# A fused transformer layer on one core: modulation computed a tile of features at a time, with keys and queries between the tiles

## The chip, the core and the metric

The kernel runs on one core of one Trainium2 chip. The core has five engines with instruction queues of their own: TensorE (PE in the profile, with PEld for its weight loads), VectorE (DVE), ScalarE (ACT), GpSimd (POOL) and SyncE (SP), which here only issues DMAs. Each engine works through its queue in order, and semaphores hold an instruction back until what it needs is there. The metric is the device time of one execution in microseconds (us). The kernel before took a median of 1546.04 us in 3 runs, 1545.74 to 1547.45.

## The reference, cut to what matters

One layer takes 256 latent tokens `x` and 256 context tokens `ctx`, each with 2048 features, in float32. The part around the change:

```python
mod = (jax.nn.silu(c) @ w_mod[l] + b_mod[l])[:, None, :]
sa, ca, ga, sm, cm, gm = jnp.split(mod, 6, axis=-1)
mod_c = jax.nn.silu(c_ctx) @ w_mod[l] + b_mod[l]
sa_c, ca_c, ga_c, sm_c, cm_c, gm_c = jnp.split(mod_c, 6, axis=-1)
h_c = modulate(x_ctx, norm_attn_w[l], sa_c, ca_c)   # rmsnorm(x, w) * (1 + scale) + shift
k_c = rmsnorm(split_qk(p_c_kv[..., :QK_WIDTH]), k_norm_w[l])      # p_c_kv = h_c @ w_in[..]
h = modulate(x, norm_attn_w[l], sa, ca)
p = h @ w_in[l]
q = axial_rope(rmsnorm(split_qk(p[..., Q_OFF:K_OFF]), q_norm_w[l]), row, col)
k = axial_rope(rmsnorm(split_qk(p[..., K_OFF:V_OFF]), k_norm_w[l]), row, col)
```

After that come values, attention, a pooling mixer, gates, an output product and an MLP of width 8192. No product of `h` can start for a block of 128 features before the shift `sa` and the scale `ca` of that block are known, and these are a product of a vector with 2048 x 256 weights.

## The kernel before, in words

**Precision.** A weight chunk is 128 x 1024 float32 (512 KB). For the large products it is split into a high part (`whi`, or `first` for the first keys; a cast on ACT, L212) and a low part (`wlo`; a subtraction on DVE, L213), and every product is three matmuls (L240 to L242, or L414 to L417 further on). The weights of the modulation are used as they were loaded.

**The first stage** makes the modulation and, beside it, the first 512 columns of keys and queries. It is `layer` from `sb = bank("ssq")` to `steps(100)`.

- There are 16 tiles of 128 features (here f0 to f15). Tile f needs four chunks of `w_m`. `mod_half` (L351) multiplies two chunks on PE into the bank `mod`: four narrow matmuls a chunk, each on 32 columns of the array; a trace counts every one twice.
- `mod_rows` copies the result out (`rows`, ACT, L356), two tiles at once; `mod_columns` turns it into columns with tiny matmuls (`modT`, PE, L365), copies them (`col`, L368) and adds bias and weight on DVE (L371 to L373); `hidden` makes `hL` (latents) or `hC` (context) of the tile from them: DVE L384, ACT L385, DVE L386.
- `pair_steps` yields steps of three matmuls (128 x 512 each). A pair of tiles needs 12: four for keys of the latents ("kx"), four for queries ("q"), four for keys of the context ("kc"). `steps(n)` puts n of them between the halves of modulation.
- `square_sums` (ACT L463, DVE L464, PE L465) and `rsq` make the norms, once for `x` at the start, once for `ctx` in tile 4.

**What sets the order.** The code is recorded in program order, and a scheduler then orders each engine's queue; where `pin` is used (for a few instructions), program order is kept. Loads come from one list (`stream`, filled by `plan`), and `wchunk` runs ahead of their use by 3 chunks. All DMAs go through SP's queue, in order; a DMA that has no free buffer holds all behind it. Chunks have five buffers (tag `raw`), for `w_m` and for the rest alike. Other tags: `w2` (nine buffers of 2 KB a partition: `rows`, `hw`, `sq`), `s8` (two of 8 KB: `cv`, the vectors of the conditioning, and `prq`, the tables), `aT` (two of 4 KB; the norms `rms` in this stage).

**Later stages.** Values (`v`), more queries and keys with attention beside them, pooling, gates, the output product, the MLP. A second list of chunks (`late_gen`: `w_ga`, `w_cm`, `w_sm`, `w_gm`) is summed up on DVE beside them, at a rate set by credits that each load gives; `late_split` splits a finished sum.

Of the kernel before, what the change touches and what calls it, by code (L numbers as in the profile page):

```python
# [32 lines left out]
for _n, _w in (("ident", 128), ("c", 16), ("cc", 16), ("bsa", 16), ("bca", 16), ("nw", 16),  # L33
               ("pscale", 8), ("subln", 1), ("edge", 60)):
    PRM[_n] = (_o, _o + _w)
    _o += _w
# [12 lines left out]
def layer(ctx: ExitStack, tc, a, out):  # L49
# [5 lines left out]
    ordered = [False]  # L55

    class Engine:


        def __init__(self, engine):  # L60
            self.engine = engine

        def __getattr__(self, name):
            emit = getattr(self.engine, name)
            return (lambda *a, **k: pin(emit(*a, **k))) if ordered[0] else emit

    act, vec = Engine(nc.scalar), Engine(nc.vector)
# [13 lines left out]
    def small(name, n):  # L81
        return pool.tile([P, n], F32, tag="sm", name=name, bufs=12)
# [28 lines left out]
    def raw_chunk(src, n=1024):  # L111
        raw = pool.tile([P, n], F32, tag="raw", name="raw", bufs=5)
        nc.sync.dma_start(raw, src)
        return raw
# [14 lines left out]
    besides = {(2, 2): [("cT", 0)], (3, 0): [("cT", 1)], (3, 2): [("cT", 2)], (4, 0): [("cT", 3)], (7, 0): [("prq",)]}  # L129
    for m in range(1, 8):  # L130
        kq = (("w_k", 0, m - 1), ("w_q", 0, m - 1))
        if m == 3:
            besides[7, 1] = kq
        else:
            besides[2 * m, 1], besides[2 * m, 3] = kq[:1], kq[1:]
# [47 lines left out]
    done = [0]  # L183

    def load_next():
# [14 lines left out]
        raw = raw_chunk(src, n)  # L200
        if key[0] == "w_m":
            loaded.append((key, raw, raw))
            return
        if key[:2] == ("w_k", 0):
# [39 lines left out]
    def rsq(v, n, div, tag=None):  # L244

        mk = (lambda nm: small(nm, n)) if n <= 16 else (lambda nm: work(nm, [P, n]))
        y = pool.tile([P, n], F32, tag=tag, name=tag, bufs=2) if tag else mk("rq_y")
# [42 lines left out]
    cv = s8("cv", [P, 4, KT, 32])[:, 0]  # L290
# [3 lines left out]
    quads = pool.tile([P, 2], F32, tag="quads", name="quads")  # L294
    vec.reduce_sum(quads, ident.rearrange("p (j c) -> p c j", j=4)[:, 0:2, :], axis=AX.X)
    b1 = small("b1", 16)
    vec.tensor_scalar(b1, pr("bca"), 1.0, None, ALU.add)

# [42 lines left out]
    def mod_half(f, half, ps):  # L341

        raws = [wchunk("w_m", f, 2 * half + i, ahead=FIRST_AHEAD)[0] for i in range(2)]
        c = (f % 2) * T
        for i in range(2):
            for j in range(4):
                k = 8 * half + 4 * i + j  # L350
                pe.matmul(ps[32 * j:32 * j + 32, c:c + T], cv[:, k, :], raws[i][:, j * T:j * T + T],  # L351
                          start=k < 4, stop=k >= 12)

    def mod_rows(ps, f, n):
        rows = work("rows", [P, n * T])
        act.copy(rows, ps[:, (f % 2) * T:(f % 2) * T + n * T])  # L356
        return rows

    def mod_columns(f, rows, n):

        pt = bank("modT")
        for i in range(n):
            for a in range(2):
                o = 2 * (a * n + i)
                pe.matmul(pt[:, o:o + 2], rows[:, (2 * i + a) * P:(2 * i + a) * P + P], quads,  # L365
                          start=i + a == 0, stop=i == n - 1 and a == 1, skip_group_check=True)
        col = small("col", 8)
        act.copy(col[:, 0:4 * n], pt[:, 0:4 * n])  # L368
        c3 = col[:, 0:4 * n].rearrange("p (i c) -> p i c", c=2)
        ks = slice(f, f + n)  # L370
        vec.tensor_add(c3[:, 0:n, :], c3[:, 0:n, :], b1[:, ks].unsqueeze(2).broadcast_to([P, n, 2]))  # L371
        vec.tensor_mul(c3[:, 0:n, :], c3[:, 0:n, :], pr("nw")[:, ks].unsqueeze(2).broadcast_to([P, n, 2]))
        vec.tensor_add(c3[:, n:2 * n, :], c3[:, n:2 * n, :], pr("bsa")[:, ks].unsqueeze(2).broadcast_to([P, n, 2]))  # L373
        return c3

    def hidden(k, t, c3, n=2):

        src, h = ((xT, hL), (cT, hC))[t]
        hw = work("hw", [P, n, T])
        for kk in range(n):  # L380
            ht, k8 = h[(k + kk) // 8], (k + kk) % 8
            u = hw[:, kk, :]
            bias = c3[:, n + kk, t:t + 1]
            vec.scalar_tensor_tensor(u, src[:, k + kk, :], c3[:, kk, t:t + 1], rms[t], ALU.mult, ALU.mult)  # L384
            act.activation(ht[:, 0, k8, :], u, AF.Identity, bias=bias)  # L385
            vec.scalar_tensor_tensor(ht[:, 1, k8, :], u, bias, ht[:, 0, k8, :].bitcast(F32), ALU.add, ALU.subtract)  # L386
# [36 lines left out]
    def qk_evac(ps, tt, g, dest, tab, wait):  # L423
# [9 lines left out]
        m1 = work("qm1")  # L433
        m3 = m1.rearrange("p (h d) -> p h d", d=64)
        if tt < 2:
            vec.tensor_mul(m3, r3, tabs[:, tab, tt, :].unsqueeze(1).broadcast_to([P, 8, 64]))
            m2 = work("qm2")
            for ax in range(2):
                for b in range(2):
                    o = ax * 32 + b * 16  # L440
                    i = ax * 32 + (1 - b) * 16
                    vec.tensor_mul(m2.rearrange("p (h d) -> p h d", d=64)[:, :, o:o + 16], r3[:, :, i:i + 16],
                                   tabs[:, tab + 1, tt, o:o + 16].unsqueeze(1).broadcast_to([P, 8, 16]))
            gp.tensor_add(m1, m1, m2)
        else:
            vec.tensor_mul(m3, r3, wkt.unsqueeze(1).broadcast_to([P, 8, 64]))

        def turn():
            pt = bank("qkT")
            for i in range(4):  # L450
                pin(pe.transpose(pt[:, i * P:i * P + P], m1[:, i * P:i * P + P], ident))
# [32 lines left out]
    order = [("kx", 0), ("q", 0), ("kx", 1), ("q", 1), ("kc", 0), ("kc", 1), ("kx", 2), ("q", 2)]  # L484
    for j in range(3, 8):
        order += [("kc", j - 1), ("kx", j), ("q", j)]
    side = chain(*(pair_steps(*o) for o in order + [("kc", 7)]))

# [4 lines left out]
    def hold(w, j):  # L493
        held[w, j] = wchunk(w, 0, j, ahead=FIRST_AHEAD)
# [3 lines left out]
    def columns(ps, f, n):  # L498
        cols[f] = mod_columns(f, mod_rows(ps, f, n), n)

# [3 lines left out]
    rms = [rsq(sb[:, 0:T], T, P / D, "aT")]  # L504
    ps = bank("mod")
    for f in range(2):
        mod_half(f, 0, ps)
        if f == 1:
            columns(ps, 0, 1)
            hidden(0, 0, cols[0], 1)  # L510
        mod_half(f, 1, ps)
    before = mod_rows(ps, 1, 1)
    for m in range(1, 8):
        f = 2 * m
        ps = bank("mod")
        if m == 2:
            sb = bank("ssq")
        mod_half(f, 0, ps)
        n = 1 if m == 1 else 2
        cols[f - n] = mod_columns(f - n, before, n)  # L520
        hidden(f - n, 0, cols[f - n], n)
        if m != 3:
            hold("w_k", m - 1)
        if m == 3:
            hidden(2, 1, cols[2])
        steps(4 if m > 2 else 0)
        mod_half(f, 1, ps)
        if m != 3:
            hold("w_q", m - 1)
        if m == 2:  # L530
            for i in range(3):
                square_sums(cT, vec, sb, i)()
        if m > 3:
            hidden(f - 2, 1, cols[f - 2])
        steps(4 if m == 3 else 3)
        mod_half(f + 1, 0, ps)
        if m == 2:
            square_sums(cT, vec, sb, 3)()
            rms.append(rsq(sb[:, 0:T], T, P / D, "aT"))
        if m == 3:  # L540
            hold("w_k", 2)
            hold("w_q", 2)
            hidden(4, 1, cols[4])
        steps(4 if m == 3 else 3)
        if m == 7:
            columns(ps, 14, 1)
            hidden(14, 0, cols[14], 1)
        mod_half(f + 1, 1, ps)
        if m == 2:
            for i in range(2):  # L550
                hidden(i, 1, cols[i], 1)
        if m == 5:
            tables()
        if m < 7:
            steps(4 if m == 3 else 2)
            before = mod_rows(ps, 0, 2)
    columns(ps, 15, 1)
    hidden(15, 0, cols[15], 1)
    hold("w_k", 7)
    hold("w_q", 7)  # L560
    steps(2)
    for i in range(2):
        hidden(14 + i, 1, cols[14 + i], 1)
    steps(100)
# [52 lines left out]
    def late_split(acc, norm_w, o):  # L617
        for q in range(2):
            ah, al = work("ah", dt=F32R), work("al", dt=F32R)
            split(ah, al, acc[:, q * 512:q * 512 + 512])  # L620
            later(4 + q, partial(late_sum, ah, al, norm_w[q] if norm_w else None, o[:, q * 512:q * 512 + 512]))
# [411 lines left out]
def _layout(inp):  # L1033
# [37 lines left out]
    for w in WINDOWS:  # L1071
# [8 lines left out]
          "edge": np.broadcast_to(edge, (P, len(edge)))}  # L1080
# [36 lines left out]
```

## Time and profile before

| what | value |
|---|---|
| median of 3 runs | 1546.04 us |
| the profiled execution | 1545.81 us |
| its span, first to last instruction | 1543.3 us |
| mean granted clock of TensorE | 0.983 |
| PE busy | 1498.7 us, 97% of the span |
| DVE, ACT busy | 987.3 us (64%), 691.3 us (45%) |
| HBM read | 344.44 MB, 225 GB/s over the span |

The profile lists instructions with start and duration. A matmul's duration includes time in the pipeline, so consecutive matmuls overlap: what one costs is the distance from its start to the next one's start. "[1.20 <-ACT first L212]" behind an instruction says that the engine sat idle for 1.20 us before it, until the instruction of that name ended. A view by windows gives, for each stretch, the busy time of every engine, then the clock that was granted to TensorE (1.00 is full), the busy share of the DMA engines and what they moved in GB/s. A view of waits sums up who waited for whom.

### The profile page before, as it was taken

How to read it: one execution, taken by the hardware profiler on the slowest of the kernel's cores; microseconds unless marked ns; L12 is line 12 of the kernel's file. 1: busy time of each engine (PE TensorE's matmuls, PEld its weight loads, DVE VectorE, ACT ScalarE, POOL GpSimd, SP SyncE). 2: the span in 40 equal slices, each digit the busy share in tenths (PEclk: the TensorE clock that was granted, in tenths of full speed). 3: DMA queues.
4: the chain of work that ended last, by engine and by line, in shares of the span. 5: the costliest groups of instructions: out<-in, count | busy, mean ns of one | idle time of the engine just before them, and what ended most of it. 6: DMA issues, size and time to landing. Idle time of an engine off the chain costs nothing.

```text
span 1543.3 us, 20017 instructions
## 1 busy us (share of the span) xinstructions
PE 1498.7 (97%) x7592; PEld 1200.3 (78%) x7592; DVE 987.3 (64%) x1215; ACT 691.3 (45%) x944; POOL 120.5 (8%) x120
## 2 busy tenths in 40 slices
PE   6898999999999999999999999999999999999998
PEld 3554787768878888888879988888888888888887
DVE  2533778778877667666767665666666555555565
ACT  3322534556555434444444554544445453444432
POOL 0000011001240000000000100100000010000260
PEclk8898999999999999999999999999999999999999
DMA  9887578455658777788765777767777556566564
GB/s 366 289 292 250 191 237 281 152 177 192 201 175 305 245 263 262 247 280 286 232 191 169 227 237 242 230 213 238 231 240 227 201 187 185 189 189 188 183 190 137
DMA packets 97439, 347.84 MB, mean 225 GB/s; under 512 B 11072, under 2 KB 11712, under 8 KB 97344
## 3 DMA queue, kind: packets, MB, share of 16 engines
q1 hardware_dynamic: 96768, 345.49, 68.2%
q8 instruction: 59, 0.97, 0.2%
q0 software_dynamic: 576, 1.08, 0.2%
q14 instruction: 36, 0.29, 0.1%
HBM read 344.44 MB, written 2.10 MB: 225 GB/s over the span
## 4 chain that ended last, share of the span: by engine, by line
PE 94%; DVE 2%; ACT 2%; POOL 1%; DMA 1%; issue 1%; DVEq 0%; SPq 0%; ACTq 0%; POOLq 0%
PE f L966 14%; PE f L414 8%; PE f L417 8%; PE f L415 8%; PE f L969 7%; PE pg L417 4%; PE pg L415 4%; PE pg L414 4%; PE mod L351 2%; PE wo L415 2%; PE pyy L415 2%; PE v L417 2%; PE pyy L417 2%; PE wo L417 2%; PE v L415 2%; PE v L414 2%
## 5 line engine op out<-in xcount | busy, mean ns | idle before, releaser
L213 DVE TENSOR_TENSOR wlo<-raw,whi 128x1024 fp32r<-128x1024 f32 x443 | 547.5, 1237 | 377.7 <-ACT whi L212 361.3
L212 ACT CAST whi<-raw 128x1024 fp32r<-128x1024 f32 x443 | 462.6, 1045 | 594.1 <-PE f L415 188.1
L966 PE MATMUL f<-h,whi 128*128 128x512 f32 x896 | 226.9, 395 | 0.0
L414 PE MATMUL f<-whi,act 128*128 128x512 f32 x512 | 202.7, 396 | 0.0
L415 PE MATMUL f<-whi,act 128*128 128x512 f32 x512 | 201.7, 394 | 0.0
L966 PEld LDWEIGHTS f<-h,whi 128*128 128x128 f32 x896 | 160.9, 188 | 30.5
L615 DVE SCALAR_TENSOR_TENSOR macc<-raw,sil,macc 128x1024 f32<-128x1024 f32 x128 | 167.2, 1306 | 1.8 <-issue 1.6
L417 PE MATMUL f<-wlo,act 128*128 128x512 f32 x512 | 140.2, 395 | 0.0
L969 PEld LDWEIGHTS f<-h,wlo 128*128 128x128 f32 x896 | 122.5, 188 | 10.2
L969 PE MATMUL f<-h,wlo 128*128 128x256 f32 x896 | 124.5, 281 | 0.0
L417 PEld LDWEIGHTS f<-wlo,act 128*128 128x128 f32 x512 | 96.0, 187 | 23.5
L414 PEld LDWEIGHTS f<-whi,act 128*128 128x128 f32 x512 | 96.0, 187 | 23.4
L415 PEld LDWEIGHTS f<-whi,act 128*128 128x128 f32 x512 | 95.9, 187 | 22.8
L414 PE MATMUL pg<-whi,hL 128*128 128x512 f32 x256 | 101.6, 397 | 0.0
L415 PE MATMUL pg<-whi,hL 128*128 128x512 f32 x256 | 101.4, 396 | 0.0
L977 POOL TENSOR_TENSOR rsq<-relu 128x512 f32<-128x512 f32 x28 | 29.2, 1042 | 547.1 <-ACT relu L976 536.9
L417 PE MATMUL pg<-wlo,hL 128*128 128x512 f32 x256 | 70.2, 395 | 1.6 <-DVE wlo L213 1.6
L417 PEld LDWEIGHTS pg<-wlo,hL 128*128 128x128 f32 x256 | 47.9, 187 | 13.7 <-DVE wlo L213 2.0
L415 PEld LDWEIGHTS pg<-whi,hL 128*128 128x128 f32 x256 | 48.0, 188 | 11.8 <-issue 0.2
L414 PEld LDWEIGHTS pg<-whi,hL 128*128 128x128 f32 x256 | 48.0, 187 | 11.4 <-issue 0.2
L415 PE MATMUL wo<-whi,mix 128*128 128x512 f32 x128 | 50.7, 396 | 0.0
L414 PE MATMUL wo<-whi,mix 128*128 128x512 f32 x128 | 50.4, 394 | 0.0
(263 smaller groups left out, 2146.7 us busy)
## 6 DMA issues: line engine op xcount, KB each, us to landing
raw<-in_w_ff_dram SPq DMA_DIRECT2D x240, 512.0 KB, 4.2
raw<-in_w_m_dram SPq DMA_DIRECT2D x64, 512.0 KB, 4.9
raw<-in_w_ga_dram SPq DMA_DIRECT2D x32, 512.0 KB, 4.4
raw<-in_w_cm_dram SPq DMA_DIRECT2D x32, 512.0 KB, 4.5
raw<-in_w_gb_in_dram SPq DMA_DIRECT2D x32, 512.0 KB, 4.5
raw<-in_w_ga_in_dram SPq DMA_DIRECT2D x32, 512.0 KB, 4.6
raw<-in_w_sm_dram SPq DMA_DIRECT2D x32, 512.0 KB, 4.6
raw<-in_w_o_dram SPq DMA_DIRECT2D x32, 512.0 KB, 4.4
```

Source lines behind the costliest of these rows:

```text
L212: act.copy(hi, raw)
L213: vec.tensor_sub(lo, raw, hi.bitcast(F32))
L351: pe.matmul(ps[32 * j:32 * j + 32, c:c + T], cv[:, k, :], raws[i][:, j * T:j * T + T], start=k < 4, stop=k >= 12)
L414: pe.matmul(banks[t], tok(h, k, 0, tt), wt, start=k == 0, stop=False)
L415: pe.matmul(banks[t], tok(h, k, 1, tt), wt, start=False, stop=False)
L417: pe.matmul(banks[t], tok(h, k, 0, tt), wt, start=False, stop=k == 2 * nk - 1)
L615: pin(vec.scalar_tensor_tensor(acc, raw, sil[:, 0, k:k + 1], acc, ALU.mult, ALU.add))
L966: pe.matmul(ps, hi[:, kk * P:kk * P + P], both(h2, k), start=k == 0, stop=False)
L969: pe.matmul(ps[:, T:2 * T], lo[:, kk * P:kk * P + P], act_slice(h2, k, 0), start=False, stop=k == KT - 1)
L977: gp.tensor_mul(sq, r, r)
```

## The change

- **Modulation.** `mod_half` becomes `mod_tile`: all four chunks of a tile in one run. Rows, columns and hidden are made for one tile, no longer for two.
- **Steps.** `PACE` sets how many steps follow each tile: none for f0 and f1, then 4, 4, 6, 6, 8, 8, and 6 from f8 on. Half of them come ahead of `mod_columns`, half behind. The last 12 steps come at the end, interleaved.
- **Order on PE.** PE's instructions of this stage keep program order (`ordered_pe`; the wrapper shows as L67).
- **Buffers.** Chunks of odd tiles go into tiles that later stages use: two into one `s8` tile, two into the two `aT` tiles. Even tiles stay in `raw`, with the chunks of keys and queries. `cv` and the two `rms` move to `w2`.
- **Squares of ctx** are all in tile 4, behind its four chunks. `hidden` of the context is caught up in f4, f5 and f6, then runs with the tile.
- **Small things.** `quads` comes with the parameters; a bias needs two operations on DVE, not three; in `qk_evac` the rotated product is made in place, in two `w2` buffers, not four; `late_split` makes its second half two chunks later; the last pair of the stage runs ahead by one chunk, not three.

PE's queue, where the scheduler had put one pair of tiles. `mod` is the modulation, `modT` its turn into columns; `w_k_254` to `w_k_257` are the banks of keys (latents, then context), `w_q_283` and `w_q_284` those of queries. Before, from the middle of f10 on:

```order
L351 MATMUL mod<-raw,cv 32x256 x4
L240 MATMUL w_k_254<-first,hL_96 128x512
L240 MATMUL w_k_255<-first,hL_96 128x512
L240 MATMUL w_k_256<-first,hC_98 128x512
L351 MATMUL mod<-raw,cv 32x256 x4
L240 MATMUL w_k_257<-first,hC_98 128x512
L241 MATMUL w_k_254<-first,hL_96 128x512
L242 MATMUL w_k_254<-first,hL_96 128x512
L241 MATMUL w_k_255<-first,hL_96 128x512
L242 MATMUL w_k_255<-first,hL_96 128x512
L351 MATMUL mod<-raw,cv 32x256 x4
```

After, one whole tile (f10), where the banks of keys are 249 and 250 and those of queries 316 and 317:

```order
L67 MATMUL mod<-raw,cv 32x256 x16
L67 MATMUL w_k_249<-first,hL_93 128x512 x3
L67 MATMUL w_k_250<-first,hL_93 128x512 x3
L67 MATMUL w_k_249<-first,hL_93 128x512 x3
L67 MATMUL modT<-prm,rows 128x2 x2
L67 MATMUL w_k_250<-first,hL_93 128x512 x3
L67 MATMUL w_q_316<-whi,hL_93 128x512
L67 MATMUL w_q_316<-wlo,hL_93 128x512
L67 MATMUL w_q_316<-whi,hL_93 128x512
L67 MATMUL w_q_317<-whi,hL_93 128x512
L67 MATMUL w_q_317<-wlo,hL_93 128x512
L67 MATMUL w_q_317<-whi,hL_93 128x512
```

Four chunks stood in four places and now stand in one; in the whole stage the 64 chunks stood in 49 places and now stand in 16.

ACT's queue, where an odd tile's rows are copied and the next chunks of keys (`first`) and queries (`whi`) are cast. Before, a pair of tiles in the second half of the stage:

```order
L356 COPY rows<-mod 128x512
L368 COPY col<-modT 128x8
L385 ACTIVATE hL_96<-hw,col 128x256 x2
L385 ACTIVATE hC_98<-hw,col 128x256
L212 CAST first<-raw 128x1024
L385 ACTIVATE hC_98<-hw,col 128x256
L212 CAST whi<-raw 128x1024
```

After, the odd tile f11:

```order
L366 COPY rows<-mod 128x256
L224 CAST first<-raw 128x1024
L376 COPY col<-modT 128x4
L224 CAST whi<-raw 128x1024
L389 ACTIVATE hL_93<-hw,col 128x256
L389 ACTIVATE hC_95<-hw,col 128x256
```

The cast of the keys stood behind the hidden tiles and now stands ahead of the columns, right behind the rows of the odd tile.

SP's queue, with buffer numbers and with what each DMA waits for (PE, DVE: an earlier reader of the buffer; DMAHW: an earlier DMA). Before, a pair of tiles:

```order
L113 DMA raw_704<-in_w_k_dram 128x1024 [waits DMAHW7_49,PE_49]
L113 DMA raw_725<-in_w_m_dram 128x1024 [waits DMAHW0_49,PE_49]
L113 DMA raw_727<-in_w_m_dram 128x1024 [waits DMAHW1_49,PE_49]
L113 DMA raw_754<-in_w_q_dram 128x1024 [waits DMAHW2_49,PE_49]
L113 DMA raw_772<-in_w_m_dram 128x1024 [waits DMAHW3_49,PE_49]
L113 DMA raw_774<-in_w_m_dram 128x1024 [waits DMAHW4_49,DVE_49]
L113 DMA raw_784<-in_w_m_dram 128x1024 [waits DMAHW5_49,PE_49]
L113 DMA raw_802<-in_w_m_dram 128x1024 [waits DMAHW6_49,PE_49]
```

After, keys and queries of one pair, then f12 (four chunks) and the start of f13:

```order
L115 DMA raw_873<-in_w_k_dram 128x1024 [waits DMAHW4_49,PE_49]
L115 DMA raw_877<-in_w_q_dram 128x1024 [waits DMAHW5_49,DVE_49]
L212 DMA raw_883<-in_w_m_dram 128x1024 [waits DMAHW6_49,PE_49]
L212 DMA raw_903<-in_w_m_dram 128x1024 [waits DMAHW7_49,PE_49]
L212 DMA raw_905<-in_w_m_dram 128x1024 [waits DMAHW0_49,PE_49]
L212 DMA raw_941<-in_w_m_dram 128x1024 [waits DMAHW4_49,DMAHW1_49,DVE_49]
L212 DMA raw_943<-in_w_m_dram 128x1024 [waits DMAHW2_49]
L212 DMA raw_943<-in_w_m_dram 128x1024 [waits DMAHW3_49]
```

Nearly every chunk of `w_m` waited for PE. Now an odd tile's chunks (943) need no reader in the same pair, and an even tile's fourth chunk (941) waits for DVE: for the subtraction that ends the use of the keys' chunk 873.

The diff, cut to its core:

```diff
     for f in range(KT):
         for i in range(4):
             plan("w_m", f, i)
-            for key in besides.get((f, i), ()):
-                plan(*key)
-    plan("w_k", 0, 7)
-    plan("w_q", 0, 7)
+            if f in (2, 3) and i % 2 == 1:
+                plan("cT", 2 * f - 4 + i // 2)
...
+        j = 2 if f == 6 else -1 if f == 5 or f % 2 == 0 else f // 2
+        if j >= 0:
+            plan("w_k", 0, j)
+            plan("w_q", 0, j)
...
+    def mod_raw(f, i):
+        if f % 2 == 0:
+            return pool.tile([P, 1024], F32, tag="raw", name="raw", bufs=5)
+        if i > 1:
+            return pool.tile([P, 1024], F32, tag="aT", name="raw", bufs=2)
+        if i == 0:
+            wide[0] = s8("raw", [P, 2, 1024])
+        return wide[0][:, i, :]
...
-    def mod_half(f, half, ps):
-        raws = [wchunk("w_m", f, 2 * half + i, ahead=FIRST_AHEAD)[0] for i in range(2)]
+    def mod_tile(f, ps):
+        raws = [wchunk("w_m", f, i, ahead=FIRST_AHEAD)[0] for i in range(4)]
         c = (f % 2) * T
-        for i in range(2):
+        for i in range(4):
             for j in range(4):
-                k = 8 * half + 4 * i + j
+                k = 4 * i + j
                 pe.matmul(ps[32 * j:32 * j + 32, c:c + T], cv[:, k, :], raws[i][:, j * T:j * T + T],
...
+    PACE = (0, 0, 4, 4, 6, 6, 8, 8) + (6,) * 8
+    context = {4: (0, 1), 5: (2, 3, 4), 6: (5, 6)}
+    ordered_pe[0] = True
...
+    for f in range(KT):
+        if f % 2 == 0:
+            ps = bank("mod")
+        rows = mod_tile(f, ps)
+        if f == 4:
             sb = bank("ssq")
+            for i in range(4):
                 square_sums(cT, vec, sb, i)()
+            rms.append(rsq(sb[:, 0:T], T, P / D, "rms"))
+        if j >= 0:
+            for w in ("w_k", "w_q"):
+                held[w, j] = wchunk(w, 0, j, ahead=FIRST_AHEAD if j < 7 else 1)
+        steps(PACE[f] // 2)
+        cols[f] = mod_columns(f, rows)
+        steps(PACE[f] - PACE[f] // 2)
+        hidden(f, 0, cols[f])
+        for k in context.get(f, (f,) if f > 6 else ()):
+            hidden(k, 1, cols[k])
...
+    lasts = [pair_steps(n, 7) for n in ("kx", "q", "kc")]
+    for _ in range(2):
+        for g in lasts:
+            next(g)
+            next(g)
+    ordered_pe[0] = False
```

More of the change, by code (lines that the diff above doesn't have):

```diff
@@ L125, in plan @@
         stream.append(((name,) + idx, rate))
[L129 to L135, printed above, removed]
     for f in range(KT):
@@ L374, in mod_columns, with hidden @@
         return c3
-    def hidden(k, t, c3, n=2):
+    def hidden(f, t, c3):
         src, h = ((xT, hL), (cT, hC))[t]
[L379 to L386, printed above, removed]
+        u = work("hw", [P, T])
+        ht, k8 = h[f // 8], f % 8
+        bias = c3[:, 1, t:t + 1]
+        vec.scalar_tensor_tensor(u, src[:, f, :], c3[:, 0, t:t + 1], rms[t], ALU.mult, ALU.mult)
+        act.activation(ht[:, 0, k8, :], u, AF.Identity, bias=bias)
+        vec.scalar_tensor_tensor(ht[:, 1, k8, :], u, bias, ht[:, 0, k8, :].bitcast(F32), ALU.add, ALU.subtract)
@@ L557, in layer @@
[L557 to L564, printed above, removed]
+    rms = [rsq(sb[:, 0:T], T, P / D, "rms")]
+    for f in range(KT):
[3 more added lines that the diff above has]
+        if f == 4:
+            sb = bank("ssq")
+            for i in range(4):
+                square_sums(cT, vec, sb, i)()
+            rms.append(rsq(sb[:, 0:T], T, P / D, "rms"))
+        j = 2 if f == 6 else -1 if f == 5 or f % 2 == 0 else f // 2
+        if j >= 0:
[7 more added lines that the diff above has]
+            hidden(k, 1, cols[k])
+        if f == 10:
+            tables()
```

152 lines of the change are left out of this document (52 added, 100 removed).

## The prediction, made before the changed kernel ran

> **What bounds the kernel now.** The sum is made against the profiled execution, 1545.81 us, of which the span is 1543.3 and 2.5 lie around it; the median of the runs shown is 0.23 above it. I began with the windows of the first stage. After the two times stand the length, then busy us (and instructions) of PE, PEld, DVE, ACT and POOL, then the clock, the DMA share and GB/s.
>
> ```profile
> 0.00:20.00 20.00, 10.26 (x73) 6.68 (x77) 5.62 (x19) 8.91 (x15) 1.82 (x6) 0.95 0.90 340
> 20.00:40.00 20.00, 16.76 (x114) 8.10 (x108) 4.97 (x12) 4.12 (x7) 0.00 (x0) 0.71 1.02 396
> 120.00:140.00 20.00, 17.53 (x108) 9.47 (x108) 5.51 (x13) 4.31 (x8) 0.00 (x0) 0.83 0.75 253
> 400.00:500.00 100.00, 92.76 (x493) 77.26 (x492) 79.83 (x99) 55.46 (x83) 23.14 (x34) 1.00 0.71 234
> ```
>
> PE is the bound of the whole, and nearly everywhere it is already full. The first stage is the exception. Up to 40 us the DMA engines are full (share 1.02). At 120 to 140 us nothing is: PE idles at a clock of 0.83, and DMA moves 253 GB/s. Two views of waits, over 0 to 171 us (us in total, times, longest), and the first row of the values, which follow the stage, say why:
>
> ```profile
> PE w_k L240 <- ACT first L212: 15.1, 6, 3.9
> ```
>
> ```profile
> SPq L113 <- PE mod L351: 87.4, 54, 4.4
> ```
>
> ```profile
> 170.80 0.40 PE L414 MATMUL v<-whi,hL 128*128 128x512 f32 x1
> ```
>
> PE waits for the keys' split, which stands on ACT behind the hidden tiles of two features at once. Meanwhile SP's queue waits 87.4 us for PE to free buffers. So each waits for the other, and the stage ends at 170.80 us. Only this start can move much.
>
> **The change, part by part.** First the price of PE's work at full clock, from three places of PE's timeline (start, duration):
>
> ```profile
> 67.66 0.39 PE L242 MATMUL w_k<-first,hC 128*128 128x512 f32 x1
> 67.98 1.07 PE L351 MATMUL mod<-raw,cv 128*32 128x256 f32 x16
> 68.98 0.50 PE L240 MATMUL w_k<-first,hC 128*128 128x512 f32 x1
> 69.32 0.40 PE L241 MATMUL w_k<-first,hC 128*128 128x512 f32 x1
> ...
> 71.64 0.39 PE L242 MATMUL w_k<-first,hC 128*128 128x512 f32 x1
> ```
>
> ```profile
> 93.31 0.40 PE L241 MATMUL w_q<-wlo,hL 128*128 128x512 f32 x1
> 93.64 0.64 PE L351 MATMUL mod<-raw,cv 128*32 128x256 f32 x8
> 94.21 0.50 PE L242 MATMUL w_q<-whi,hL 128*128 128x512 f32 x1
> 94.54 0.39 PE L242 MATMUL w_k<-first,hC 128*128 128x512 f32 x1
> ```
>
> ```profile
> 154.03 0.39 PE L242 MATMUL w_q<-whi,hL 128*128 128x512 f32 x1
> 154.26 0.50 PE L365 MATMUL modT<-quads,rows 128*128 128x2 f32 x4
> 154.62 0.48 PE L240 MATMUL w_q<-whi,hL 128*128 128x512 f32 x1
> 154.93 0.40 PE L241 MATMUL w_q<-wlo,hL 128*128 128x512 f32 x1
> ```
>
> From 69.32 to 71.64 there are ten matmuls: 0.232 us each, so a step of three is 0.70. From 67.66 to 69.32 are 1.66 us; less two ordinary matmuls (0.46), two chunks of modulation cost 1.20. From 93.31 to 94.54, one chunk costs 0.77. So a chunk is 0.43, and each interruption of the wide matmuls is 0.34. Before, 64 chunks stood in 49 places; now in 16. That alone is 33 x 0.34 = 11.2 us less PE work. A tile's four chunks cost 4 x 0.43 + 0.34 = 2.06. A tile's columns (modT) cost 154.93 - 154.03 - 0.46 = 0.44, about half of what a pair costs at once, so making them singly is free. A tile with six steps is 2.06 + 18 x 0.232 + 0.44 = **6.68 us**, with eight 8.07.
>
> The order on PE puts half of the steps, 2.1 us, between a tile's chunks and its columns, which covers the copy of its rows, and more than 5 us between the columns and the keys that need the hidden tile. So PE's 15.1 us of waits for keys go. What is late next? Three things: DMA at the start, the squares in f4, and the even tiles' fourth chunk. Their prices come from the groups of the stage (mean ns ahead of the second bar) and the landing of a chunk (last number, us):
>
> ```profile
> L213 DVE TENSOR_TENSOR first<-raw,first 128x1024 fp32r<-128x1024 f32 x8 | 9.8, 1222 | 0.7 <-ACT first L212 0.7
> L212 ACT CAST first<-raw 128x1024 fp32r<-128x1024 f32 x8 | 8.3, 1038 | 0.8 <-DMA raw<-in_w_k_dram 0.8
> L463 ACT ACTIVATE sq<-cT 128x512 f32<-128x512 f32 x8 | 4.5, 617 | 0.0
> L356 ACT COPY rows<-mod 128x256 f32<-128x256 f32 x4 | 1.5, 372 | 15.5 <-PE mod L351 15.5
> ```
>
> ```profile
> raw<-in_w_m_dram SPq DMA_DIRECT2D x37, 512.0 KB, 4.5
> ```
>
> *Start.* Up to the end of f3, the parameters, `xT`, 16 chunks of `w_m`, `cT`, and one of keys and of queries must land: 13.8 MB. The windows give 340 and 396 GB/s, so 14.7 MB by 40 us, and 13.8 by 37.7. The changed queue loads the same things there, so I cost it alike. f3 is done at 38.3. f4's fourth chunk waits for the subtraction of the second keys, which now stands behind f3's hidden tile: two slow steps 2.6, columns and hidden about 2.8 (an estimate from the durations above), cast and subtraction 2.3, landing 4.5. f4 is done at about 51.
>
> *Squares.* ACT takes them behind f4's rows: 0.37, eight times 0.617, then the last addition and its matmuls, about 1.9: 7.2 us in which PE, in program order, can do nothing else. Before, much of that lay beside other work. At 58.2 the steps go on.
>
> *Fourth chunk.* SP's rows show that f12's fourth chunk waits for the keys' subtraction, and ACT's that the keys' cast stands behind the odd tile's rows. From the end of f11's chunks: rows 0.37, cast 1.04, subtraction 1.22, hand-offs 0.4, landing 4.5: 7.5 us. PE meanwhile has six steps and columns, 4.62, and three chunks of f12, 1.43: 6.05. So PE waits **1.5 us**, in f10, f12 and f14: 4.5. SP's queue is held in the meantime, but what stands behind it (the odd tile's chunks) is due 6 us later. Bounds: nothing, if the chunk lands in 3.0; 2.2 us a time more, if the wait lowers the clock (below).
>
> *Sum.* 58.2 + 4.62 (f4's steps) + 6.68 (f5) + 2 x 8.07 (f6, f7) + 8 x 6.68 (f8 to f15) + 36 x 0.232 (the last steps) + 4.5 = **152 us** for the first matmul of the values, against 170.80: 18.9 less.
>
> *DMA as the bound.* A pair of tiles needs ten chunks, 5.24 MB, in 2 x 6.68 + 1.5 = 14.9 us: 352 GB/s. What it reached with PE at work:
>
> ```profile
> 32.00:40.00 8.00, 6.51 (x55) 3.64 (x55) 1.23 (x1) 0.59 (x1) 0.00 (x0) 1.00 1.03 418
> 78.00:84.00 6.00, 6.00 (x42) 4.40 (x41) 1.28 (x6) 1.59 (x4) 0.00 (x0) 1.00 0.99 363
> ```
>
> So DMA just suffices; it is no bound of its own, but has no slack at the lower row.
>
> *At nothing.* The products in place in `qk_evac`, the bias and the earlier rows lie beside PE's matmuls of the values, 24 x 0.232 = 5.6 us a chunk. Two chunks of values in place of three ahead leave 11 us for the third's landing, cast and subtraction (6.8). Without that cover it would be up to 6.8, once. The second list now runs about three chunks earlier, and its sums are split in two moves. That reorders DVE where PE idles, 400 to 500 us (100 - 92.76 = 7.2 us). A chunk that falls better or worse there is worth at most about that, either way; I take 0, as total DVE work stays. Result: 1545.8 - 18.9 = **1527 us**.
>
> **The clock.** Whether a wait of 1.5 us lowers it, the trace answers both ways:
>
> ```profile
> 160.13 0.74 PE L240 MATMUL w_k<-first,hL 128*128 128x512 f32 x2 [1.20 <-ACT first L212]
> ...
> 163.11 0.63 PE L241 MATMUL w_k<-first,hL 128*128 128x512 f32 x1
> 163.54 0.63 PE L242 MATMUL w_k<-first,hL 128*128 128x512 f32 x1
> ...
> 164.78 0.39 PE L242 MATMUL w_k<-first,hL 128*128 128x512 f32 x1
> ```
>
> ```profile
> 418.03 0.66 PE L692 MATMUL aTp<-prm,e 128*128 128x128 f32 x4 [2.47 <-DVE d L787]
> ...
> 418.65 0.28 PE L241 MATMUL pin<-hL,whi 128*128 128x256 f32 x1
> 418.77 0.28 PE L242 MATMUL pin<-hL,wlo 128*128 128x256 f32 x1
> ```
>
> After 1.20 us the pitch is 0.43 until 164.78: of 4.65 us, 46% are lost, 2.1. After 2.47 us it stays full (0.12 for half the columns). The first wait came behind tiny matmuls, the second amid dense ones. The new wait lies amid dense ones, so I take full clock. [...]
>
> **Rivals.**
> 1. *The wait lowers the clock*: three times 2.1 us, so 1533. For it, the row at 160; against, that at 418.
> 2. *No wait, and the later idle shrinks*: the fourth chunk lands sooner (-4.5), and up to 6 of the 7.2 us go: 1517 to 1522. Against: 4.5 us is the median landing.
> 3. *DMA becomes the bound, and the kernel slower.* If it stays at the 253 GB/s of 120 to 140 us, then from 17.0 MB at 50 us, the last modulation chunk (45.6 MB) lands at 163, and 0.6 + 4.62 + 8.35 behind it give 177: 1552. The point is 267 GB/s, where the stage ends at 170.8. Against: SP's 87.4 us show that buffers, not the engines, held the 253.
> 4. *The change doesn't do what it says*: chunks are bunched, but PE waits for them at both tiles of a pair, with the slow clock, so that 11 to 12 us more are lost between f4 and f15 than in rival 1; 1543 to 1549, no difference.
>
> **How the numbers follow.** Forecast 0.46 (1522 to 1531 with its bounds), rival 1 0.24 (1531 to 1539), rival 2 0.16 (1514 to 1522), rival 4 0.07, rival 3 0.07. Predicted: 1527. From 1517 to 1539 lie the forecast, rival 1 and most of rival 2, a little over 0.8. 0.2% is 3 us, about what a measurement of this kernel can tell from no change. Faster: 0.46 + 0.24 + 0.16 = 0.86; same 0.07; slower 0.07.
>
> **What would show it.** Right: values from about 152 us; sixteen modulation groups of 1.9 to 2.1 us; 33 groups fewer; from 70 to 145 us a clock of 1.00 and 340 to 360 GB/s; three waits of `mod` for DMA near 1.5 us; no waits for `first`; a gap of 5 to 7 us near 51 at the squares. Wrong: waits for `raw` in odd tiles, windows under 1.00 behind f8, DMA under 300 GB/s, or PE idle grown between 400 and 500 us.

## The result and the profile after

| | before (4 runs) | after (4 runs) |
|---|---|---|
| median | 1546.74 us (1545.74 to 1547.45) | 1507.73 us (1506.33 to 1508.80) |
| ratio | | 0.9748, 95% interval 0.9731 to 0.9765 |
| the profiled execution, its span | 1545.81, 1543.3 | 1506.33, 1504.5 |
| mean granted clock | 0.983 | 0.991 |

The kernel is 39 us faster; 19 were predicted, and the time lies 9 us below the range. One execution of e5, further down, is left out everywhere: it took 1648.33 us at a granted clock of 0.841, where e5's others had 0.982 to 0.985.

The windows of the kernel after, over the stretches that were shown of before (columns as there):

```profile
0.00:20.00 20.00, 10.81 (x76) 6.35 (x76) 6.68 (x20) 9.40 (x16) 1.82 (x6) 1.00 0.93 356
20.00:40.00 20.00, 13.04 (x97) 6.35 (x98) 5.01 (x10) 4.33 (x9) 0.00 (x0) 0.74 1.02 403
120.00:140.00 20.00, 19.70 (x159) 14.04 (x152) 10.01 (x20) 8.24 (x16) 0.00 (x0) 1.00 0.96 366
400.00:500.00 100.00, 95.32 (x463) 79.56 (x462) 79.59 (x92) 53.46 (x73) 18.12 (x26) 0.99 0.79 257
```

The row at 120 is the one to read: PE is busy for 19.70 of 20 us at full clock, where it was 17.53 at 0.83, and DMA moves 366 GB/s instead of 253. The waits of the kernel after up to 148 us, PE's and then SP's queue (us in total, times, longest), and the first matmul of the values:

```profile
PE mod L67 <- DMA raw<-in_w_m_dram: 13.5, 16, 3.0
PE ssq L67 <- DVE sq L466: 9.6, 2, 7.2
PE modT L67 <- ACT rows L366: 1.0, 2, 0.5
```

```profile
SPq L212 <- DMA raw<-in_w_k_dram: 22.8, 5, 5.2
SPq L212 <- PE mod L67: 12.0, 6, 9.9
```

```profile
147.97 0.39 PE L418 MATMUL v<-whi,hL 128*128 128x512 f32 x1
```

The 15.1 us of waits for the keys' split are gone, and SP's 87.4 us for `mod` are 22.4 (12.0, and 10.4 under a second line). The values start at 147.97, 22.8 us earlier than before.

Fewer waits are the smaller part of that. Two other waits of PE grew; before, they were:

```profile
PE ssq L465 <- DVE sq L464: 7.1, 1, 7.1
PE mod L351 <- DMA raw<-in_w_m_dram: 4.5, 5, 1.6
```

All listed waits of PE in the stage fell from 27.5 us to 24.1. The larger part is PE's busy time, which fell by 19.6 us at a higher mean clock (0.87, then 0.94). The whole stage, of the kernel before and then of the kernel after:

```profile
0.00:170.60 170.60, 143.20 (x896) 83.31 (x897) 66.18 (x161) 55.53 (x101) 1.82 (x6) 0.87 0.83 294
0.00:147.70 147.70, 123.62 (x895) 83.77 (x896) 67.98 (x157) 57.22 (x112) 1.82 (x6) 0.94 0.90 341
```

But the span is 38.8 us shorter, so **16 us come from behind the first stage**, where the prediction had nothing. They have no window of their own. They show in the distance between starts in PE's timeline, here in the MLP, of the kernel before and then of the kernel after:

```profile
1002.92 1.10 PE L417 MATMUL f<-wlo,act 128*128 128x512 f32 x4
1003.86 0.40 PE L414 MATMUL f<-whi,act 128*128 128x512 f32 x1
1004.09 0.39 PE L415 MATMUL f<-whi,act 128*128 128x512 f32 x1
...
1005.72 1.10 PE L417 MATMUL f<-wlo,act 128*128 128x512 f32 x4
```

```profile
1002.30 1.07 PE L421 MATMUL f<-wlo,act 128*128 128x512 f32 x4
1003.20 0.39 PE L418 MATMUL f<-whi,act 128*128 128x512 f32 x1
1003.43 0.39 PE L419 MATMUL f<-whi,act 128*128 128x512 f32 x1
...
1005.02 1.07 PE L421 MATMUL f<-wlo,act 128*128 128x512 f32 x4
```

From one group of four to the next are twelve matmuls: 2.80 us before, 2.72 after, that is 233 ns and 227 ns apiece. Nothing waits in either piece, the clock is 1.00 in both (windows 1002 to 1006), and the diff doesn't touch this code. Behind the stage there are some 3700 of this width, and their distances add up to 863 us before and 839 after.

What differs is where the operands lie. The change lets `quads` come with the parameters, and so a tile of 8 bytes, which took 32 bytes of every partition, is gone; what was allocated behind it moves down. From the built programs, start in bytes of a partition:

```
                            before                 after
whi (streamed)      200192 = 64 x 3128       200160 = 64 x 3127 + 32
wlo (streamed)      212480 = 64 x 3320       212448 = 64 x 3319 + 32
act (loaded)         34016 = 64 x 531 + 32    34016
```

In a 128x512 matmul of the later stages `whi` or `wlo` (512 columns) is streamed and a 128x128 block of `hL` or `act` is loaded ahead of it (`LDWEIGHTS` on PEld, 0.19 us each in the traces of both kernels). In the matmuls that are 256 or 2 x 256 columns wide it is the other way round: a 128x128 block of `whi` or `wlo` is loaded, and `hL`, `h2` or the like is streamed. All tiles of that kind (tag `s16`) start at 224 beyond a multiple of 256.

### The profile page after: what moved, and what is told of

Its sections match the earlier page's. It is cut to its first block, busy times and chain, and to the rows that moved or that the text cites. A ratio compares the mean times of both kernels' runs of the same rounds, so it can differ in the third digit from the quotient of the medians.

```text
span 1504.5 us, 20036 instructions
## 1 busy us (share of the span) xinstructions
PE 1457.1 (97%) x7592; PEld 1205.5 (80%) x7592; DVE 992.0 (66%) x1216; ACT 694.6 (46%) x956; POOL 120.7 (8%) x120
## 4 chain that ended last, share of the span: by engine, by line
PE 87%; DVE 4%; DMA 4%; ACT 2%; issue 1%; POOL 1%; SPq 0%; DVEq 0%; ACTq 0%; POOLq 0%
PE f L940 14%; PE f L419 8%; PE f L418 8%; PE f L421 8%; PE f L943 7%; PE pg L419 3%; PE pg L418 3%; PE pg L421 3%; DMA raw<-in_w_m_dram 2%; PE w_k L67 2%; PE wo L419 2%; PE wo L421 2%; PE wo L418 2%; PE pyy L418 2%; PE pyy L419 2%; PE pyy L421 2%
## 5 line engine op out<-in xcount | busy, mean ns | idle before, releaser
L418 PE MATMUL f<-whi,act 128*128 128x512 f32 x512 | 199.4, 389 | 0.0
L419 PE MATMUL f<-whi,act 128*128 128x512 f32 x512 | 199.3, 389 | 0.0
L421 PE MATMUL f<-wlo,act 128*128 128x512 f32 x512 | 136.8, 389 | 0.0
L943 PEld LDWEIGHTS f<-h,wlo 128*128 128x128 f32 x896 | 122.3, 190 | 8.7
L421 PEld LDWEIGHTS pg<-wlo,hL 128*128 128x128 f32 x256 | 48.0, 188 | 12.3 <-DVE wlo L225 2.4
```

Source lines behind the costliest of these rows:

```text
L418: pe.matmul(banks[t], tok(h, k, 0, tt), wt, start=k == 0, stop=False)
L419: pe.matmul(banks[t], tok(h, k, 1, tt), wt, start=False, stop=False)
L421: pe.matmul(banks[t], tok(h, k, 0, tt), wt, start=False, stop=k == 2 * nk - 1)
L943: pe.matmul(ps[:, T:2 * T], lo[:, kk * P:kk * P + P], act_slice(h2, k, 0), start=False, stop=k == KT - 1)
```

## Experiments on the addresses

Each kernel has one or two tiles more that nothing reads or writes; the instructions and their order are those of the kernel named. First, 32 bytes:

```diff
@@ e1 (before) @@
     quads = pool.tile([P, 2], F32, tag="quads", name="quads")
+    pool.tile([P, 8], F32, tag="pad", name="pad")
@@ e2 (after) @@
     sub8 = pool.tile([P, 1], F32, tag="sub8", name="sub8")
+    pool.tile([P, 8], F32, tag="pad", name="pad")
@@ e4 (after), e5 (before) @@
+    pool.tile([P, 8], F32, tag="pad", name="pad")
     prm = pool.tile([P, PRM_W], F32, tag="prm", name="prm")
```

> The kernel before with one unused tile of 32 bytes a partition right behind `quads`: everything from the small columns on (the chunks `raw`, the high and low parts `whi` and `wlo`) starts 32 bytes further on, at 32 instead of 0 beyond a multiple of 64 bytes, as in the kernel after; `act`, `hL`, `first` and the instructions stay. Address theory (the distance from one 128x512 matmul's start to the next, 234 ns before and 227 after, comes from where the weights lie): the 128x512 rows behind the first stage go to 227 ns, some 3000 matmuls by 7 ns, and the time falls by about 20 us to 1523 to 1529 us; the 256-wide ones go from 117 to 120. Order theory (the distance comes from fewer waits or the new order on PE): 234 ns stays and the time is that of before, 1545 to 1548.

> The kernel after with one unused tile of 32 bytes a partition behind `sub8`: `raw`, `whi` and `wlo` lie at multiples of 64 bytes again, as in the kernel before, `act`, `hL` and `first` stay at 32 beyond one. Address theory: 128x512 matmuls behind the first stage go back to 234 ns, and the time to 1525 to 1531 us, so that of the 39 us gained some 19 to 22 are the addresses' and the rest the first stage's. Order theory: 227 ns stays, 1506 to 1509 us.

> The kernel after with the 32 bytes ahead of everything: `whi` and `wlo` lie at multiples of 64 bytes and `act`, `hL`, `first` too. Of the address theory there are two forms. Weights alone (a 128x512 matmul is slow when its weights start at a multiple of 64): 234 ns everywhere, `first` included, 1526 to 1532 us. Both operands (slow when weights and moving operand lie differently to 64 bytes): all agree, 227 ns, 1506 to 1510. Order theory: 1506 to 1509.

> The kernel before with the 32 bytes ahead of everything: `whi` and `wlo` at 32 beyond a multiple of 64 bytes, `act`, `hL` and `first` at multiples. Weights alone: 227 ns behind the first stage, 1523 to 1529 us, with the rows on `first` at 234. Both operands: they differ as in the kernel before, 234 ns, 1545 to 1548. Order theory: 1545 to 1548.

Measured: e1 1529.16 us (ratio to before 0.9872, 0.9854 to 0.9890), e2 1528.78 (0.9881, 0.9866 to 0.9896), e4 1504.71 (0.9729, 0.9709 to 0.9750), e5 1546.76 (0.9996, 0.9986 to 1.0005). e1 and e4 lie 0.2 and 1.3 us outside the ranges of the theory that they bear out. The order theory falls: 32 unused bytes take 18 us from the kernel before and give 21 to the kernel after. So does the form with one operand alone: in e4 the chunks lie at multiples of 64, as in the kernel before, and it is fast (227.0 ns for 128x512); in e5 they lie 32 beyond one, as in the kernel after, and it is slow (233.3 ns). What counts in these four runs is how the two operands lie to each other.

Whether 64 bytes are the whole rule was asked of the next four, by pads ahead of `raw` (it moves both parts) and between `whi` and `wlo`. In m1 they move the parts by 64 and 96 bytes; in m2 by 64 and 128, in m3 by 192 and 256, in m4 by 320 and 384:

```diff
@@ m1 (after) @@
     sub8 = pool.tile([P, 1], F32, tag="sub8", name="sub8")
+    pool.tile([P, 16], F32, tag="pad", name="pad")
...
+            if ("w_q", 0, 0) == key:
+                pool.tile([P, 8], F32, tag="pad2", name="pad2")
             lo = pool.tile([P, n], F32R, tag="wlo", name="wlo", bufs=3)
```

> The kernel after with `whi` 64 bytes and `wlo` 96 bytes further on. Written as where `act` and `hL` start less where the weights start, modulo 512 bytes: the kernel before and e2, e5 had 224 (234 ns for 128x512 and 117 for 256 wide), after and e4 had 256 (227 and 120), e1 had 192 (229 and 113). Here `whi` has 192 and `wlo` 160. If only the 64 bytes count (same or not), `whi` keeps 227 and `wlo` goes to 234 in the same kernel. If the difference modulo 512 counts, `whi` rows go to 229 and those with `wlo` to something new; 256-wide rows of `pin`, `f<-h` fall to 113 or 114. Time 1500 to 1515. If neither address counts, 227 and 1507 stay.

> The kernel after with `whi` 64 and `wlo` 128 bytes further on: the starts of `act`, `hL` and of both parts agree modulo 64 bytes; `act` less chunk is 192 and 128 modulo 512. 64-byte theory: no group of 128x512 matmuls near 234 ns, `whi` at 226 to 229 and `wlo` likewise, where the run with 64 and 96 had `wlo` at 234. Rival (what counts is some other distance, say the one between `whi` and `wlo`): `wlo` stays at 231 to 235. Time by the first 1500 to 1511, by the second about 1520.

> The kernel after with `whi` 192 and `wlo` 256 bytes further on (`act` less chunk 64 and 0 modulo 512). 64-byte theory: 226 to 229 for 128x512, time 1500 to 1511; what is left open is whether the 256-wide groups stand at 113 as in e1 or at 120 as in the kernel after.

> The kernel after with `whi` 320 and `wlo` 384 bytes further on (`act` less chunk 448 and 384 modulo 512). 64-byte theory: 226 to 229 for 128x512, time 1500 to 1511; the 256-wide groups between 113 and 120.

Measured: 1523.70, 1521.36, 1522.98 and 1520.74 us. The 64-byte theory said 1500 to 1511 for the last three and missed; for m1, 1500 to 1515 was expected, which missed too. What m1 does show, within one kernel, is that the two parts differ when their places differ:

```profile
1001.40 0.40 PE L421 MATMUL f<-whi,act 128*128 128x512 f32 x1
...
1003.01 0.39 PE L422 MATMUL f<-whi,act 128*128 128x512 f32 x1
1003.24 1.10 PE L424 MATMUL f<-wlo,act 128*128 128x512 f32 x4
1004.18 0.40 PE L421 MATMUL f<-whi,act 128*128 128x512 f32 x1
```

From 1001.40 to 1003.24 are eight matmuls on `whi`: 230 ns each. From 1003.24 to 1004.18 are four on `wlo`, whose distance from `act` is an odd multiple of 32 (160): 235 each. But an odd multiple of 32 isn't needed for that: in m3 the matmuls on `whi`, 64 from `act`, take 233.2 ns in the mean. And m2 and m4, which differ by 256 bytes, have the same times per matmul within 0.5 ns, so the period looked like 256. The last four asked that, with one pad, and one of them put the kernel after's distance into the kernel before:

```diff
@@ n1 (after; n2: 32 in place of 64, n4: 16; n5: before, 120) @@
     sub8 = pool.tile([P, 1], F32, tag="sub8", name="sub8")
+    pool.tile([P, 64], F32, tag="pad", name="pad")
```

> The kernel after with `whi` and `wlo` both 256 bytes further on: `act` and `hL` less chunk is 0 modulo 512, where the kernel after has 256. If the period is 256 bytes, nothing changes: 227 ns for 128x512, 120 for 256 wide, 1504 to 1510 us. If it is 512, 128x512 leaves 227 (229 to 234), 1515 to 1530.

> The kernel after with `whi` and `wlo` both 128 bytes further on, so that the two agree with each other and stand 128 from `act` and `hL` modulo 256. If all three must agree modulo 256: 229 to 232 ns for 128x512, 1512 to 1523 us. If it is enough that `whi` and `wlo` agree with each other (and all modulo 64): 227, 1504 to 1510.

> The kernel after with `whi` and `wlo` both 64 bytes further on, the distance that e1 had (192). If the distance alone sets it: 229 ns for 128x512, 113 to 115 for 256 wide, as in e1, and a time of 1503 to 1511, since the two differences nearly cancel. If what else the kernels differ in counts too, 256 wide stays at 117 to 120, and 1510 to 1518.

> The kernel before with `whi` and `wlo` 480 bytes further on: the distance of 256 that the kernel after has, in the program of before. Address theory: 227 ns for 128x512, 119 to 120 for 256 wide, 1524 to 1530 us; what is left to 1507.7 is the first stage's. Against it: 1545 to 1548.

Measured: n1 1506.86 us (0.9731, 0.9707 to 0.9755), n2 1526.75 (0.9867, 0.9850 to 0.9883), n4 1508.67 (0.9742, 0.9727 to 0.9756), n5 1521.70 (0.9829, 0.9814 to 0.9843). n1 and n4 are inside what was expected; n2 lies 4 us above the nearer of its two ranges, n5 2 us below its own. All from the traces, with the mean distance from a matmul's start to the next one's (those under 300 ns, from the first matmul of the values on), where `whi` or `wlo` is an operand:

```
start of act less start of    mean ns, and number, of matmuls     us
whi / wlo, modulo 256        512 wide  2 x 256 wide  256 wide   in all  kernels
                             (3697)       (896)       (1702)
  0 /   0                     227.0       229.9       121.5    1252   n5 (after, e4, n1: 227.0)
192 / 192                     229.0       232.7       116.4    1252   e1 (n4: 229.0)
192 / 128                     230.5       232.5       121.5    1265   m2 (m4: 230.5)
192 / 160                     231.6       233.1       121.3    1271   m1
 64 /   0                     232.5       230.1       121.5    1272   m3
128 / 128                     232.7       232.7       121.7    1276   n2
224 / 224                     233.3       232.9       120.3    1276   before (e5: 233.3, e2: 233.2)
```

The same distance gives the same figures in either program: for 512 columns to 0.1 ns (n5 and after, e1 and n4), for 256 columns within 1 ns (121.5 and 122.3, 116.4 and 117.0). 256 bytes more change nothing (n1: 227.0 ns, 1506.86 us against 1507.73). Of the distances tried, equal starts modulo 256 gave the shortest time for 512 columns (227.0). A distance of 192 costs 2 ns there and saves 5 on 256-wide matmuls, which cancels (1252 us both). The longest came at half a period (232.7), at 224 (233.3) and at 64 in m3 (233.2 on `whi`).

The distance of one pair isn't everything, though. In m3 `wlo` lies equal to `act`, and yet its 512-wide matmuls take 230.9 ns, not 226.7 as in the kernel after; there `whi` lies elsewhere. In m2 `whi` is at 192 as in e1, and takes 230.1 instead of 228.9. Nor does `raw` stand still in these runs: it moves with `whi`. Why the steps are as they are isn't shown by these runs. The rule is also not complete: in the first stage the matmuls on `first`, which agrees with `hL` and `hC` in every kernel, stood at 227 to 229 ns in the kernel after and at 231 to 232 in before and n5; and in n4, which moves only what lies behind `sub8` of the kernel after, those on `first` with `hC` stood at 231.3 instead of 226.9. And e1 is 7 us slower than n5 with the same sum, since its first stage ends later (values from 176.3 instead of 169.7 us); why is open.

n5 splits the gain: **addresses 26 us** (1547.84 to 1521.70; the sums of distances give 24, from 1276 to 1252), **all the rest 14** (1521.70 to 1507.73). The profiled executions take the rest apart: 21.7 us are won in the first stage (values from 169.70, then 147.97), and 7.2 are lost behind it (from the first matmul of the values to the end it is 1349.3 us in n5 and 1356.5 in the kernel after). So all of the 16 us from behind the stage, and more, are the addresses'.

## Experiments on the first stage

Two parts of the change were undone, one at a time and together:

```diff
@@ s2 (after) @@
-    ordered_pe[0] = True
@@ s1 (after; s4: both) @@
-        if f % 2 == 0:
+        if f < KT:
             return pool.tile([P, 1024], F32, tag="raw", name="raw", bufs=5)
```

> The kernel after without program order on PE in the first stage: the scheduler spreads the modulation over 46 places instead of 16, all else stays (addresses, odd tiles' chunks in the later stages' tiles). By the prediction's own term each interruption costs 0.34 us: 30 x 0.34 = 10.2 us, so the first matmul of `v` at about 158 instead of 148.0 and a time of about 1518 (1514 to 1522). Rival: PE waited for transfers in any case, and the interruptions lie inside those waits: 148 to 151, 1506 to 1511.

> The kernel after with all chunks of the modulation in `raw` (five buffers), the order on PE as in after. Buffer theory (SP waits for PE to free `raw`, so transfers start late and PE waits for `mod`): the stage loses much of what it gained, first `v` at 158 to 168, time 1517 to 1528, DMA in 70 to 140 us below 320 GB/s. Order theory (the gain is that the modulation stands in 16 places): first `v` at 148 to 152, time 1506 to 1512.

> The kernel after without program order on PE in the first stage (49 places of modulation, as in the kernel before) and with all its chunks in `raw`. One alone cost 21.6 us of the stage (order; first `v` at 169.6) or 12 (buffers; 160.0). If they are independent, first `v` at about 181 and a time of 1536 to 1542. If the late loads and the split groups are one and the same loss (whichever is later holds the other), 169 to 173, 1526 to 1531.

| | chunks all in `raw` | odd tiles in the later stages' tiles |
|---|---|---|
| scheduler's order | s4: values from 171.05, 1527.21 us | s2: 169.84, 1526.58 |
| program order | s1: 160.24, 1518.76 | after: 147.97, 1507.73 |

s1 lies where its buffer theory put it, and s4 where one loss hides the other; s2 lies at neither of its two places (about 158, or 148 to 151). The order alone gives 10.8 us (171.05 to 160.24), the buffers alone 1.2, and both 23.1. The largest waits of PE that part the versions, in s2 and then in s1:

```profile
PE w_k L252 <- ACT first L224: 7.0, 5, 2.8
PE modT L373 <- ACT rows L366: 3.4, 7, 0.5
```

```profile
PE mod L67 <- DMA raw<-in_w_m_dram: 18.9, 23, 3.4
```

With the scheduler's order PE still waits for the keys' split, whatever the buffers (7.0 us in s2, 7.6 in s4); with program order and `raw` alone it waits for chunks. Here too, waits are the smaller part: all that are listed up to the values come to 26.2 us in s2, 29.0 in s1 and 24.1 in the kernel after. PE's busy time there is 143.16 us in s2 (mean clock 0.90), 130.91 in s1 (0.90) and 123.62 in the kernel after (0.94). How much of the difference is the clock and how much the interruptions was not taken apart. The windows of s2, s1 and, above, the kernel after at the same place:

```profile
120.00:140.00 20.00, 17.51 (x112) 9.56 (x112) 6.66 (x16) 5.16 (x12) 0.00 (x0) 0.91 0.69 266
```

```profile
120.00:140.00 20.00, 16.68 (x137) 9.91 (x134) 7.91 (x17) 5.62 (x12) 0.00 (x0) 0.97 0.90 329
```

266, 329 and 366 GB/s; s4 moves 277 there. With the scheduler's order the buffers raise nothing (277 without them, 266 with them), and with program order they do (329, 366): they pay only once PE takes a tile's chunks at once.

One more edit was undone, for the waits behind the stage:

```diff
@@ s3 (after; qk_evac as before) @@
+        m1 = work("qm1")
+            m2 = work("qm2")
-            gp.tensor_add(raw, raw, sq)
+            gp.tensor_add(m1, m1, m2)
```

> The kernel after with `qk_evac` as before (the rotated product in buffers of its own, four `w2` buffers, POOL's addition into `qm1`). Behind the stage the kernel after waits some 5 us longer than before, the addresses aside (`qkT` for POOL 2.8 us, `pin` for `wlo` 4.3, `sc` 2.9; before has none of the first). If the in-place product makes the transposes late, 2 to 4 us go: 1504 to 1506. If those waits come from the earlier start of the stage, the time stays within 2 us of 1507.7 and the `qkT` wait with it.

Measured: 1504.02 us (0.9723, 0.9705 to 0.9742). The time fell as the first theory said, but the wait that should have gone stayed, 3.5 us instead of 2.8:

```profile
PE qkT L455 <- POOL qm L448: 3.5, 3, 1.6
```

And e4 and n1, which do the work of the kernel after, lie at 1504.71 and 1506.86. So the product in place isn't shown to cost anything. The kernel after's rows of waits stand against those of n5, which is before's program with the same matmul distances (behind the stage, kernel after, then n5):

```profile
PE pin L254 <- DVE wlo L225: 4.3, 2, 2.9
PE h2T L882 <- DVE yt L67: 4.2, 1, 4.2
PE qkT L453 <- POOL qraw L446: 2.8, 3, 1.3
PE sc L647 <- ACT e L652: 2.0, 1, 2.0
```

```profile
PE h2T L909 <- DVE yt L65: 4.2, 1, 4.2
PE aTp L693 <- DVE d L788: 2.4, 1, 2.4
```

The kernel after has 18.6 us of listed waits there, n5 12.3. The largest single one, 2.86 us at 398, has a chunk's subtraction behind sums of the second list, on DVE:

```profile
395.42 1.28 DVE L581 SCALAR_TENSOR_TENSOR macc<-raw,sil,macc 128x1024 f32<-128x1024 f32 x1
396.62 0.41 DVE L761 SCALAR_TENSOR_TENSOR d<-za,pin 128x256 f32<-128x256 f32 x1
396.95 1.22 DVE L225 TENSOR_TENSOR wlo<-raw,whi 128x1024 fp32r<-128x1024 f32 x1
```

That the second list's place among the chunks causes this is read from the rows only; the old `late_split` in the new kernel wasn't tried. The earlier end of the stage is not the cause. In s4 the values start at 171.05, as late as before, and its waits behind the stage are those of the kernel after, 18.6 us in all, these among them:

```profile
PE pin L254 <- DVE wlo L225: 4.3, 2, 2.9
PE qkT L453 <- POOL qraw L446: 2.8, 3, 1.3
PE sc L646 <- ACT e L651: 2.0, 1, 2.0
```

No version beat the kernel after beyond the intervals: s3, e4 and n1 lie 1 to 4 us below it, and theirs overlap with it.

## Why the prediction was wrong

*Start and squares: right to 1 us, by two misses that nearly cancel.* f4's last chunk was done at 49.1 (said: about 51), the squares then held PE for 8.4 us (said: 7.2), and the steps went on at 57.50 (said: 58.2).

```profile
48.50 0.64 PE L67 MATMUL mod<-raw,cv 128*32 128x256 f32 x8 [2.01 <-DMA raw<-in_w_m_dram]
51.49 6.35 PE L67 MATMUL ssq<-sq,mean 128*128 128x256 f32 x16 [2.35 <-DVE sq L466]
57.50 2.42 PE L67 MATMUL w_k<-first,hL 128*128 128x512 f32 x9
```

*A tile with six steps: right.* 6.68 us were worked out; from f8 to f9 it is 91.54 - 84.92 = 6.62:

```profile
84.92 1.94 PE L67 MATMUL mod<-raw,cv 128*32 128x256 f32 x32
91.54 1.93 PE L67 MATMUL mod<-raw,cv 128*32 128x256 f32 x32
```

*Fourth chunk: right in place, too large.* The waits stand in f10, f12 and f14 as said, for the cause said (in f12 the keys' subtraction ended at 109.87 and the DMA left SP's queue at 109.89), but they are 0.30, 0.65 and 0.30 us: 1.3 instead of 4.5. In f12 the chain put at 7.5 us took 7.05, and PE's work beside it, put at 6.05, took 6.40. Of that, three chunks were put at 1.43 us; by the prediction's own prices they come to 3 x 0.43 + 0.34 = 1.63.

```profile
99.96 0.64 PE L67 MATMUL mod<-raw,cv 128*32 128x256 f32 x8 [0.30 <-DMA raw<-in_w_m_dram]
114.20 0.64 PE L67 MATMUL mod<-raw,cv 128*32 128x256 f32 x8 [0.65 <-DMA raw<-in_w_m_dram]
127.96 0.64 PE L67 MATMUL mod<-raw,cv 128*32 128x256 f32 x8 [0.30 <-DMA raw<-in_w_m_dram]
```

That is the larger part of the 4 us by which the stage ended earlier than the 152 that were summed up.

*The rivals.* Rival 1 didn't come about: the waits left the clock at 1.00, but they are too short to say what 1.5 us would have done. Rival 3 fell at 366 GB/s (346 from 70 to 145 us, where 340 to 360 were said), rival 4 at the 22.8 us. Rival 2 was nearly right on the waits (1.3 us, not none) and wrong on the idle behind, which grew: from the values on PE was idle for 17.2 us before and for 23.3 after.

*The interruptions.* 33 x 0.34 = 11.2 us of PE work: the order alone gave 10.8. That is partly luck: from s4 to s1 PE's busy time fell by 12.6 us (143.54 to 130.91), and its listed waits rose by 1.8 (27.2 to 29.0). The same price for s2, 10.2 us, missed by half: its values start 21.9 us later than the kernel after's. PE is busy for 19.5 us more there, at a clock of 0.90 instead of 0.94, and the waits for the split are back.

*At nothing: the step that failed.* All that lies behind the stage was costed at 0. Two things stand there instead. The first is `quads`: its removal isn't in the prediction's list of things at nothing, and was put at 0 without a reason. It moved the chunks by 32 bytes, the 512-wide matmuls behind the stage went from 233.3 to 227.0 ns, and that was 26 us (n5 against before; 24 by the sums of distances). The second is PE's waits behind the stage, which grew by about 6 us (18.6 against 12.3). That is inside the 7.2 on either side that the prediction had named and then taken as 0, but not where it named them: from 400 to 500 us PE idles for 4.7 us, less than before, and the new idle time stands ahead of it (6.2 us from 148 to 300 and 2.9 from 300 to 400, where n5 has 0.0, from 170, and 0.5). The price of 0.232 us isn't what failed: its rows are matmuls on `first`, whose place the diff didn't change. What failed is to take it that matmuls whose code the diff leaves alone keep their price; the diff changed where their operands lie.

e2, the kernel after with the old distance between the operands, gave 1528.78 us, 18.8 less than before, against the 18.9 and 1527 of the sum. That agreement is partly luck: its stage had 22.3 of them (values from 148.54), so two errors of about 3.5 us, one in the stage and one behind it, cancel.

## What to carry to other kernels

When a diff adds, removes or resizes any on-chip tile, compare the start addresses of the matmul operands before and after, and pad to put a pair back (or in a better place) before crediting the edit itself: here 32 bytes less took the 128x512 matmuls behind the stage from 233.3 to 227.0 ns, and addresses were 26 of some 40 us (n5). If every matmul of a kind gets slower or faster by the same few nanoseconds (here 6) with no wait in sight, look at addresses first. And undo parts of a change one at a time and together: here one part paid 1 us alone and 12 beside the other.

## What the runs showed of the hardware

- The distance between the starts of dense 128x512 matmuls in this kernel changed with where the streamed and the loaded operand start relative to each other, modulo 256 bytes (n1, 256 bytes further on, kept 227.0 ns): 227.0 ns when equal, 229.0 at 192, 232.7 at 128, 233.3 at 224, with both parts of the chunk at the same distance. For 256 columns the best was 192 (116.4 and 117.0, against 120.3 to 122.3).
- An unused tile of 32 bytes changed the time of the whole kernel by 18 us (e1) and 21 us (e2); one of 480 bytes by 26 us (n5). Where all operands moved together, 32 bytes changed little or nothing (e4 1504.71 against 1507.73, e5 1546.76 against 1547.59).
